# A state-space input product as one float32r product of stacked parts, its weights prepared by a side task of its own

## The chip, the cores and the metric

The kernel runs on one core of a Trainium2 chip. The metric is the device time of one execution in microseconds (us), the median of a few runs. A matrix product on TensorE (PE) can take float32 operands, or float32r operands, which are float32 values rounded to fewer bits; a float32 matmul leaves two records in the trace, a float32r matmul one.

## The reference, cut to what matters

Two transformer-like blocks of width 2048 work on 256 tokens. The first has a feed-forward part (`ffn1`), then a mixer made of a state-space branch (64 groups of 16 channels, each driving 64 complex states) and an attention branch, then a second feed-forward part. The second block follows it. The part that changes is the input of the state space:

```
u32 = u.reshape(Bsz, S, N_SSM_GROUPS, SSM_GROUP)
bu_re = jnp.einsum('bsgh,gph->sbgp', u32, bb_re)
bu_im = jnp.einsum('bsgh,gph->sbgp', u32, bb_im)
_, _, s_re, s_im = lax.associative_scan(_ssm_combine, (a_re_t, a_im_t, bu_re, bu_im), axis=0)
y = einsum(s_re, c_re) - einsum(s_im, c_im) + d * u32
```

Here `u` is the last quarter of the columns of `hn @ w_in`, 256 tokens by 1024 channels.

## The kernel before

Nearly all of the time goes to large products with weights that stream from memory. Each float32 operand is split into two float32r parts, hi and lo, and each product is the sum of three: hi by hi, hi by lo, lo by hi (`gemm`, lines 247 to 249 with the activations stationary, 255 to 257 with the weights stationary). The weights go through a pipeline by units of 128x1024: SyncE loads `raw`, ScalarE (ACT) writes `whi` (line 106), VectorE (DVE) writes `wlo` (line 116). When `gemm` takes a unit for use, it first puts the rounding of the unit four places on into ACT's queue and the `wlo` of the unit three places on into DVE's queue. So DVE is never more than three whole units ahead of PE.

Everything else is written as side tasks, Python generators that issue some instructions and then yield. After each unit `gemm` calls `tick`: the tick number rises by one, deferred functions that are due run, and each side task in the list goes on while the sum of yielded costs stays under a budget (`share`). A yield of `(cost, lag)` also keeps the task asleep for `lag` ticks. All engines take their instructions strictly in the order in which this recording issues them. `finish(task)` runs a task to its end with no product between its steps.

The names that matter here:

- `early` is a chain of side tasks that runs under `ffn1`; behind `ffn1` stands `K.finish(*early)`, and then the products with `w_in` start, first the two for `uT` (line 993 writes it, scaled, from PSUM), then those for `qT`, `kT`, `vt`.
- `next_norm` works on the end of `ffn1`: it spills `h` by two POOL (GpSimd) DMAs for each quarter (line 913), and transposes it (`tr`, line 304) two ticks later.
- `ssm_states` is a side task, spawned behind the two `uT` products. For 16 steps `jp` it multiplies 2 x 128 states: its products `bu` (line 701) take 32 rows of `uT` by 32 rows of the weights `sB`, in plain float32; DVE turns them (lines 705 to 709), scans (714) and turns back (719 to 723), POOL adds (725, 726), and every second step `out` multiplies by C (`sy`, line 684).
- `attend1` is the attention side task, ahead of `ssm_states` in the list. It takes eight pairs of heads: scores `ap` (757), `aS` (761 to 769), transposes `apt` (779) into `aPT` (780), `ao` (790).
- Behind the context's products (`ctx_columns`, whose side tasks write `cky` and `ckt`) stands `attn_half(0)`, four ticks of products, and then `K.finish(ssm)`.
- The pool `m4` has ten buffers of 128x1024 floats, and all these tasks share it: in `ssm_states` `rot` (for this step and the next), `ssw` and `sst` of this step, and up to two older `ssw`, in all up to six; in attention and its neighbours `aS` (two), `aPT`, `cky` and `ckt`, in all five.

Of the kernel before, what the change touches and what calls it, by code (L numbers as in the profile page):

```python
# [7 lines left out]
F32 = mybir.dt.float32  # L8
F32R = mybir.dt.float32r
I32 = mybir.dt.int32  # L10
AF = mybir.ActivationFunctionType
# [5 lines left out]
P = 128  # L17
D = 2048
T = 256
# [513 lines left out]
            yield 1800  # L533


def mod_vectors(K):
    nc = K.nc
    K.cs = K.c("cs", (P, 2, 16))
    nc.gpsimd.dma_start(K.cs[:, 0], K.a["c_x"])
    nc.gpsimd.dma_start(K.cs[:, 1], K.a["c_ctx"])  # L540
    yield 0, 4
    nc.scalar.activation(K.cs[:], K.cs[:], AF.Silu)
    K.modT = K.c("modT", (P, 2, 2, 16))
    K.gate = K.dram.tile([1, D], F32, name="gate")
# [65 lines left out]
def ctx_norm(K):  # L610
    nc, v = K.nc, K.nc.vector
    K.cnorm = K.dram.tile([2, P, D], F32, name="cnorm")
    for t in range(2):
        x = K.b8("ctx")
        nc.gpsimd.dma_start(x[:], K.a["ctx"][t * 128:t * 128 + 128, :])
        yield 0, 3
        mv, r = layer_stats(K, x, "cn")
        yield 3500
        v.tensor_scalar(x[:], x[:], mv[:, 0:1], r[:], op0=OP.subtract, op1=OP.mult)
        nc.gpsimd.dma_start(K.cnorm[t], x[:])  # L620
        yield 1200
# [39 lines left out]
def ssm_states(K, uT):  # L661

    nc, v, a = K.nc, K.nc.vector, K.a
    B, C, E = {}, {}, {}

    def fetch(jp):
        if jp >= 16:
            return
        if jp % 2 == 0:
            kt = jp // 2  # L670
            B[kt] = K.t1("sB", (P, 2, 128))
            nc.gpsimd.dma_start(B[kt][:], a["s_b"][kt])
            C[kt] = K.t1("sC", (P, 2, 4, 32))
            for i in range(2):
                nc.gpsimd.dma_start(C[kt][:, i], K.cfold[i, :, 4 * kt:4 * kt + 4, :])
        E[jp] = K.m4("rot", (P, 2, 2, 256))
        nc.gpsimd.dma_start(E[jp][:].rearrange("p a b c -> p (a b c)"), K.rot[jp])

    def out(kt, ws):
        p = K.ps("sy")  # L680
        for ri in range(2):
            for j in range(4):
                q = 32 * j
                nc.tensor.matmul(p[q:q + 32, :256], C[kt][:, ri, j], ws[j // 2][:, ri, j % 2], start=ri == 0, stop=ri == 1,
                                 skip_group_check=True)
        v.scalar_tensor_tensor(uT[:, kt, :], uT[:, kt, :], K.ssd[:, kt:kt + 1], p[:, :256], op0=OP.mult, op1=OP.add)

    fetch(0)
    yield 0, 2
    ws = []  # L690
    for jp in range(16):
        kt, half = divmod(jp, 2)
        fetch(jp + 1)
        c, e = E[jp][:, 0], E[jp][:, 1]
        w, t = K.m4("ssw", (P, 2, 2, 256)), K.m4("sst", (P, 2, 2, 256))
        bs = [K.ps("bu", (P, 2, 256)) for j in range(2)]

        for ri in range(2):
            for j in range(2):
                q = 32 * (2 * half + j)  # L700
                nc.tensor.matmul(bs[j][:, ri], B[kt][q:q + 32, ri], uT[q:q + 32, kt, :], start=ri == 0, stop=True,  # L701
                                 skip_group_check=True)
        for j in range(2):
            b = bs[j]
            v.tensor_tensor(w[:, :, j], b[:], c[:, j][:, None, :].to_broadcast([P, 2, 256]), op=OP.mult)
            v.tensor_tensor(t[:, :, j], b[:], e[:, j][:, None, :].to_broadcast([P, 2, 256]), op=OP.mult)
            yield 1200
        v.tensor_sub(w[:, 0], w[:, 0], t[:, 1])
        v.tensor_add(w[:, 1], w[:, 1], t[:, 0])
        yield 1500  # L710
        for ri in range(2):
            for j in range(2):
                m = K.mag[:, 2 * jp + j:2 * jp + j + 1].to_broadcast([P, 256])
                v.tensor_tensor_scan(w[:, ri, j], m, w[:, ri, j], 0.0, op0=OP.mult, op1=OP.add)
            yield 1350
        if len(ws) == 2:
            out(kt - 1, ws)
            ws = []
        v.tensor_tensor(t[:, 0], c, w[:, 0], op=OP.mult)
        v.tensor_tensor(t[:, 1], e, w[:, 0], op=OP.mult)  # L720
        yield 1200
        v.tensor_tensor(w[:, 0], e, w[:, 1], op=OP.mult)
        v.tensor_tensor(w[:, 1], c, w[:, 1], op=OP.mult)
        yield 1200
        nc.gpsimd.tensor_add(w[:, 0], t[:, 0], w[:, 0])
        nc.gpsimd.tensor_sub(w[:, 1], w[:, 1], t[:, 1])
        del E[jp]
        ws.append(w)
        yield 100
    yield 0, 3  # L730
    out(7, ws)
    yield 300, 2
# [199 lines left out]
def constants1(K):  # L932
    nc, a = K.nc, K.a
    yield 0, 6
    for name, shape in (("ones", (P, 1)), ("mask1", (P, 384)), ("halfpi", (P, 1)), ("ssd", (P, 8)), ("glub", (P, 8)),
                        ("gain_ssm", (P, 8)), ("gain_attn", (P, 8)), ("convw", (P, 4, 16))):
        t = K.c(name, shape)
        nc.gpsimd.dma_start(t[:], a[name])
        setattr(K, name, t)


def block1(K):
    nc, v, a = K.nc, K.nc.vector, K.a
    kx = list(range(16))
    h = [K.b8(f"h{t}") for t in range(2)]
    constants(K)
    for n in range(4):
        for t in range(2):
            c = slice(n * 512, n * 512 + 512)
# [21 lines left out]
            K.defer(2 * n + 1, lambda n=n, t=t: N.add(t, n, h[t][:, n * 512:n * 512 + 512]))  # L971
    K.defer(8, lambda: R.update(n1=N.done(D)))
    K.share = 1060.0
    early = [K.spawn(chain(constants1(K), mod_vectors(K), ctx_norm(K), ssm_prep(K), mod_rows(K, (0, 1), (0, 1))))]


    K.hspill = K.dram.tile([2, P, D], F32, name="hspill")
    xT2 = {}
# [7 lines left out]
    uT, qT, kT = (K.b8(n, (P, 8, 256)) for n in ("uT", "qT", "kT"))  # L986
    vt = K.b8("vt", (P, 2, 1024))

    def keepT(dst, i):
        def ev(acc):  # L990
            for q in range(2):
                o = dst[:, 4 * i + 2 * q:4 * i + 2 * q + 2, :]
                v.tensor_tensor(o, acc[:, q].rearrange("p (a b) -> p a b", a=2), R["rb"][:, None, :].to_broadcast([P, 2, 256]),
                                op=OP.mult)
        return ev

    for dst, n0 in ((uT, 3072), (qT, 0), (kT, 1024)):
        for i in range(2):
            K.gemm("T", "w_in", kx, n0 + 512 * i, 512, xT2, keepT(dst, i))
        if dst is uT:  # L1000
            ssm = K.spawn(ssm_states(K, uT))
    cT = {}
# [861 lines left out]
def cols(g,n): return np.ascontiguousarray(np.asarray(g).reshape(n,128).T)  # L1864
# [7 lines left out]
def small(I):  # L1872
    f=np.float32
    a={"x":I["x"][0],"ctx":I["ctx_2"][0]}
    a["ident"]=np.eye(128,dtype=f); a["ones"]=np.ones((128,1),f)
    t=np.arange(256)[:,None]; s=np.arange(256)[None]; d=t-s
    c=((d>=0)&(d<=128)).astype(int)+((d>=0)&(d%4==0))+((d>=0)&(d%16==0))
    m=np.where(c>0,8*np.log(np.maximum(c,1)),-1e30).astype(f)
    a["mask1"]=np.ascontiguousarray(np.concatenate([m[:128,:128],m[128:]],1))
    a["steps"]=np.broadcast_to(np.arange(256,dtype=f),(128,256)).copy(); a["halfpi"]=np.full((128,1),np.pi/2,f)  # L1880
    a["gains"]=np.ascontiguousarray(np.stack([cols(I[n][0],16) for n in("ffn1_norm","mix_norm","ffn2_norm")],1))
    a["ssd"]=cols(I["ssm_d"][0],8); a["glub"]=cols(I["ssm_b_glu"][0],8)
    a["gain_ssm"]=cols(I["ssm_out_norm"][0],8); a["gain_attn"]=cols(I["attn_out_norm"][0],8)
    a["convw"]=np.ascontiguousarray(np.stack([cols(w,16) for w in I["conv_w_2"][0]]+[cols(I["conv_b_2"][0],16)],1))
    st=lambda x: np.ascontiguousarray(x.reshape(32,128).T)
    a["s_lr"]=st(I["ssm_a_re"][0]); a["s_li"]=st(I["ssm_a_im"][0])
    a["s_ld"]=st(np.repeat(I["ssm_log_dt"][0],64))
    for n,k in(("s_cre","ssm_c_re"),("s_cim","ssm_c_im")):
        z=np.zeros((2,64,32,2,16),f)
        C=I[k][0].reshape(32,2,16,64)  # L1890
        for g in range(2): z[g,:,:,g,:]=C[:,g].transpose(2,0,1)
        a[n]=z.reshape(128,1024)
    z=np.zeros((8,4,2,16,2,2,64),f)
    for q,k in((0,"ssm_b_re"),(1,"ssm_b_im")):
        Bm=I[k][0].reshape(8,4,2,64,16)
        for g in range(2): z[:,:,g,:,q,g,:]=Bm[:,:,g].transpose(0,1,3,2)
    a["s_b"]=z.reshape(8,128,2,128)
    a["c_x"]=cols(I["c_2"][0],16); a["c_ctx"]=cols(I["c_ctx_2"],16)
    a["b_mod"]=I["b_mod_2"][0][None]; a["w_mod"]=I["w_mod_2"][0]
    return a  # L1900
# [47 lines left out]
```

## Time and profile before

| | us |
|---|---|
| median of 3 runs | 3184.89 (3184.13 to 3186.52) |
| profiled execution, its own time | 3183.86 |
| span of its trace | 3182.1 |
| PE busy | 3160.6 (99%) |
| DVE busy | 2227.1 (70%) |
| ACT busy | 1508.0 (47%) |
| POOL busy | 266.0 (8%) |

The span is the time from the first to the last instruction in the trace; 1.8 us of the execution's own time lie around it. Busy time of PE includes overlap of pipelined matmuls, so it tells that PE hardly ever waits, not that it could not be faster.

### The profile page before, as it was taken

The numbers are of one execution on the slowest core, as the hardware profiler recorded it, in microseconds if no ns is written. First come the engines' busy times: TensorE is split into PE (matmuls) and PEld (weight loads), VectorE is DVE, ScalarE is ACT, GpSimd is POOL, SyncE is SP. The second block draws the span as 40 slices with busy tenths as digits, with TensorE's granted clock in tenths as the row PEclk, the third lists the DMA queues.
The fourth block names the chain that finished last, engine by engine and source line by source line (L and its number), as shares of the span: only waits on it lengthen the run. The fifth ranks groups of instructions, "written<-read, shape, count | busy, mean of one in ns | idle before, by whom it ended". The sixth has DMA issues, their size and how long they took to land.

```text
span 3182.1 us, 41884 instructions
## 1 busy us (share of the span) xinstructions
PE 3160.6 (99%) x16096; PEld 2676.0 (84%) x16096; DVE 2227.1 (70%) x3160; ACT 1508.0 (47%) x1980; POOL 266.0 (8%) x411
## 2 busy tenths in 40 slices
PE   8999999999999999999999999999999999999999
PEld 7888888889988788888888888889988888888887
DVE  6768798795986887665766547767656875445567
ACT  5574444444357455544444444545544444444443
POOL 1000000000231321000000000000001110000001
PEclk9999999999999999999999999999999999999999
DMA  7678677776564565565876556554445555655663
GB/s 262 241 270 285 238 272 264 259 262 212 201 231 151 185 244 184 208 206 191 306 256 237 191 192 228 206 197 174 150 161 172 182 185 202 231 182 199 220 233 133
DMA packets 117144, 684.32 MB, mean 215 GB/s; under 512 B 15611, under 2 KB 15899, under 8 KB 52171
## 3 DMA queue, kind: packets, MB, share of 16 engines
q1 hardware_dynamic: 95616, 610.90, 53.8%
q0 software_dynamic: 21328, 70.74, 6.5%
q8 instruction: 126, 2.06, 0.3%
q14 instruction: 74, 0.61, 0.1%
HBM read 646.41 MB, written 35.18 MB: 214 GB/s over the span
## 4 chain that ended last, share of the span: by engine, by line
PE 96%; DVE 2%; ACT 1%; DMA 1%; issue 0%; POOL 0%; DVEq 0%; SPq 0%; ACTq 0%; POOLq 0%
PE acc L247 27%; PE acc L249 26%; PE acc L248 26%; PE acc L255 3%; PE acc L256 3%; PE acc L257 3%; PE tr L304 1%; PE mN L1467 1%; PE o2p L1381 1%; PE s L1359 1%; DVE wlo L116 1%; DMA raw<-w_ffn_w_gate 1%; PE bu L701 0%; PE pt L1371 0%; PE acc L281 0%; PE cp L1246 0%
## 5 line engine op out<-in xcount | busy, mean ns | idle before, releaser
L116 DVE TENSOR_TENSOR wlo<-raw,whi 128x1024 fp32r<-128x1024 f32 (+2 forms) x1072 | 1300.1, 1222 | 514.0 <-PE acc L248 402.1
L106 ACT ACTIVATE whi<-raw 128x1024 fp32r<-128x1024 f32 (+2 forms) x1072 | 1112.5, 1044 | 1131.6 <-PE acc L249 898.4
L247 PE MATMUL acc<-whi,xTh 128*128 128x512 f32 (+1 forms) x1472 | 570.6, 388 | 2.0 <-ACT xTh L313 2.0
L248 PE MATMUL acc<-wlo,xTh 128*128 128x512 f32 (+1 forms) x1472 | 568.0, 386 | 0.7 <-DVE wlo L116 0.7
L249 PE MATMUL acc<-whi,xTl 128*128 128x512 f32 (+1 forms) x1472 | 567.9, 386 | 0.3 <-DVE xTl L319 0.3
L247 PE MATMUL acc<-whi,uT2h 128*128 128x512 f32 (+2 forms) x992 | 387.4, 390 | 0.0
L249 PE MATMUL acc<-whi,uT2l 128*128 128x512 f32 (+2 forms) x992 | 380.9, 384 | 0.0
L248 PE MATMUL acc<-wlo,uT2h 128*128 128x512 f32 (+2 forms) x992 | 380.4, 383 | 0.0
L247 PEld LDWEIGHTS acc<-whi,xTh 128*128 128x128 f32 x1472 | 277.1, 188 | 56.9 <-ACT xTh L313 2.8
L249 PEld LDWEIGHTS acc<-whi,xTl 128*128 128x128 f32 x1472 | 277.0, 188 | 53.3 <-DVE xTl L319 0.6
L248 PEld LDWEIGHTS acc<-wlo,xTh 128*128 128x128 f32 x1472 | 277.2, 188 | 52.9 <-DVE wlo L116 1.9
L247 PE MATMUL acc<-whi,gTh 128*128 128x512 f32 x688 | 269.6, 392 | 1.2 <-DVE h L404 1.2
L249 PE MATMUL acc<-whi,gTl 128*128 128x512 f32 x688 | 268.3, 390 | 0.0
L248 PE MATMUL acc<-wlo,gTh 128*128 128x512 f32 x688 | 268.1, 390 | 0.0
L247 PEld LDWEIGHTS acc<-whi,uT2h 128*128 128x128 f32 x992 | 186.6, 188 | 37.2 <-issue 2.5
L249 PEld LDWEIGHTS acc<-whi,uT2l 128*128 128x128 f32 x992 | 186.4, 188 | 36.8
L248 PEld LDWEIGHTS acc<-wlo,uT2h 128*128 128x128 f32 x992 | 186.7, 188 | 35.1
L572 DVE SCALAR_TENSOR_TENSOR macc<-mraw,cs,macc 128x1024 f32<-128x1024 f32 x160 | 205.2, 1282 | 4.9 <-DMA mraw<-w_mod 4.9
L247 PEld LDWEIGHTS acc<-whi,gTh 128*128 128x128 f32 x688 | 129.3, 188 | 27.7 <-ACT whi L106 1.6
L249 PEld LDWEIGHTS acc<-whi,gTl 128*128 128x128 f32 x688 | 129.2, 188 | 26.9
L248 PEld LDWEIGHTS acc<-wlo,gTh 128*128 128x128 f32 x688 | 129.3, 188 | 26.2
L247 PE MATMUL acc<-whi,wTh 128*128 128x512 f32 (+1 forms) x384 | 148.2, 386 | 0.0
(549 smaller groups left out, 4431.4 us busy)
## 6 DMA issues: line engine op xcount, KB each, us to landing
raw<-w_w_in SPq DMA_DIRECT2D x192, 1024.0 KB, 4.9
raw<-w_ffn_w_gate SPq DMA_DIRECT2D x80, 1024.0 KB, 5.1
raw<-w_ffn_w_up SPq DMA_DIRECT2D x80, 1024.0 KB, 4.9
raw<-w_ffn_w_down SPq DMA_DIRECT2D x80, 1024.0 KB, 4.9
mraw<-w_mod SPq DMA_DIRECT2D x96, 512.0 KB, 6.4
raw<-w_w_out SPq DMA_DIRECT2D x28, 1024.0 KB, 4.9
rot<-rot POOLq DMA_DIRECT2D x32, 512.0 KB, 5.2
raw<-w_w_branch_b SPq DMA_DIRECT2D x16, 1024.0 KB, 4.8
```

Source lines behind the costliest of these rows:

```text
L106: K.nc.scalar.activation(hi[:, :nu * w], raw, AF.Copy)
L116: K.nc.vector.tensor_sub(lo[:, :n], raw, hi[:, :n].bitcast(F32))
L247: nc.tensor.matmul(o, xh[:, ts], wh, start=first, stop=False)
L248: nc.tensor.matmul(o, xh[:, ts], wl, start=False, stop=False)
L249: nc.tensor.matmul(o, xl[:, ts], wh, start=False, stop=last)
L255: nc.tensor.matmul(o, wh[:, ns], xh, start=first and n % 2 == 0, stop=False, **sk)
L256: nc.tensor.matmul(o, wh[:, ns], xl, start=False, stop=False, **sk)
L257: nc.tensor.matmul(o, wl[:, ns], xh, start=False, stop=last, **sk)
L304: nc.tensor.transpose(p[:, o:o + 128], src(kt, t), self.ident[:])
L572: v.scalar_tensor_tensor(accs[row][:], w[:], K.cs[:, row, kt:kt + 1], accs[row][:], op0=OP.mult, op1=OP.add)
L1359: nc.tensor.matmul(p[:], l[:, t * 128:t * 128 + 128], kk[:, r], start=i == 0, stop=i == 2)
L1381: nc.tensor.matmul(p[:, :128], PT[:, t, s * 128:s * 128 + 128], va[:, s, g * 128:g * 128 + 128], start=s == 0, stop=s == 3)
```

## The change

`ssm_inputs_prep` is a second early side task. It sleeps 60 ticks, then takes the weights of the input product, now laid out as three copies of 32 rows by 8192 columns, in eight chunks of 96x1024: a POOL DMA loads `bx`, ACT rounds it to `bz` (all three row blocks hi), DVE overwrites the middle block by lo, and a POOL DMA stores `bz` to `bst` in memory. `keep_u` splits `uT` into `uh` and `ul` after each of its two products and stores them to `ust` in memory. `fetch` then loads for each step a tile `us` of `m4` that holds u (hi, hi, lo in rows 0, 32 and 64) and the weights (hi, lo, hi), with four POOL DMAs, in place of the one for `sB`. The product has 96 rows in float32r; each of its two halves is issued just ahead of its DVE work. The first product comes five ticks after the first fetch, where it was two.

```
+def ssm_inputs_prep(K):
+    nc, v = K.nc, K.nc.vector
+    K.bst = K.dram.tile([96, 8192], F32R, name="bst")
+    yield 0, 60
+    for c in range(8):
+        cs = slice(c * 1024, c * 1024 + 1024)
+        x, z = K.m4("bx", (96, 1024)), K.m4("bz", (96, 1024), F32R)
+        nc.gpsimd.dma_start(x[:], K.a["s_b"][:, cs])
+        yield 0, 4
+        nc.scalar.activation(z[:], x[:], AF.Copy)
+        yield 0, 1
+        v.tensor_sub(z[32:64], x[32:64], z[32:64].bitcast(F32))
+        nc.gpsimd.dma_start(K.bst[:, cs], z[:])
+        yield 1200, 8
...
-            B[kt] = K.t1("sB", (P, 2, 128))
-            nc.gpsimd.dma_start(B[kt][:], a["s_b"][kt])
...
+        U[jp] = K.m4("us", (96, 2, 512), F32R)
+        for i in range(3):
+            nc.gpsimd.dma_start(U[jp][32 * i:32 * i + 32, 0].rearrange("r (j t) -> r j t", j=2),
+                                K.ust[i // 2, jp // 2, jp % 2].rearrange("j r t -> r j t"))
+        nc.gpsimd.dma_start(U[jp][:, 1], K.bst[:, jp * 512:jp * 512 + 512])
...
     fetch(0)
-    yield 0, 2
+    yield 0, 5
...
-        bs = [K.ps("bu", (P, 2, 256)) for j in range(2)]
-        for ri in range(2):
-            for j in range(2):
-                q = 32 * (2 * half + j)
-                nc.tensor.matmul(bs[j][:, ri], B[kt][q:q + 32, ri], uT[q:q + 32, kt, :], start=ri == 0, stop=True,
-                                 skip_group_check=True)
         for j in range(2):
-            b = bs[j]
+            b = K.ps("bu", (P, 2, 256))
+            for ri in range(2):
+                o = (2 * j + ri) * 128
+                nc.tensor.matmul(b[:, ri], U[jp][:, 1, o:o + 128], U[jp][:, 0, j * 256:j * 256 + 256], start=ri == 0,
+                                 stop=True, skip_group_check=True)
...
-    early = [K.spawn(chain(constants1(K), mod_vectors(K), ctx_norm(K), ssm_prep(K), mod_rows(K, (0, 1), (0, 1))))]
+    early = [K.spawn(chain(constants1(K), mod_vectors(K), ctx_norm(K), ssm_prep(K), mod_rows(K, (0, 1), (0, 1)))),
+             K.spawn(ssm_inputs_prep(K))]
...
+        def parts():
+            ks = slice(4 * i, 4 * i + 4)
+            hi, lo = (K.m4(n, (P, 4, 256), F32R) for n in ("uh", "ul"))
+            nc.scalar.activation(hi[:], uT[:, ks], AF.Copy)
+            v.tensor_sub(lo[:], uT[:, ks], hi[:].bitcast(F32))
+            for x, z in enumerate((hi, lo)):
+                nc.gpsimd.dma_start(K.ust[x, ks].rearrange("k a j r t -> (a j r) k t"), z[:])
```

Where `ffn1` ends, POOL's queue before holds the last spills of `h` and then the first fetch of `ssm_states` (`sB`, `sC`, `rot`). Now it holds this behind the same spills (a name's number tells the buffer):

```order
L931 DMA hspill_133<-h0_83 128x512
L931 DMA hspill_133<-h1_84 128x512
L544 DMA bx_5868<-s_b 96x1024
L549 DMA bst_180<-bz_5869 96x1024
L544 DMA bx_5874<-s_b 96x1024
L549 DMA bst_180<-bz_5875 96x1024
L544 DMA bx_5880<-s_b 96x1024
L549 DMA bst_180<-bz_5881 96x1024
L544 DMA bx_5886<-s_b 96x1024
L549 DMA bst_180<-bz_5887 96x1024
L1027 DMA ust_5896<-uh_6155 128x4x256
```

Four of the eight chunks of `ssm_inputs_prep` stand here, each store ahead of the next chunk's load. On DVE the same place, between the last row of the norm of `h` and the copy of `rb`, reads before:

```order
L332 SCALAR_TENSOR_TENSOR n2ry<-n2rt,n2ry 128x2
L116 TENSOR_TENSOR wlo<-raw,whi 128x1024 x2
L319 SCALAR_TENSOR_TENSOR xTl<-tr,gains,xTh 128x256 x4
L116 TENSOR_TENSOR wlo<-raw,whi 128x1024 x3
L631 COPY rb<-row 128x256
```

and now:

```order
L332 SCALAR_TENSOR_TENSOR n2ry<-n2rt,n2ry 128x2
L548 TENSOR_TENSOR bz<-bx,bz 32x1024 x4
L116 TENSOR_TENSOR wlo<-raw,whi 128x1024
L319 SCALAR_TENSOR_TENSOR xTl<-tr,gains,xTh 128x256 x4
L116 TENSOR_TENSOR wlo<-raw,whi 128x1024 x4
L648 COPY rb<-row 128x256
```

The four subtractions of the chunks now stand ahead of the next `wlo`; on ACT the four copies stand likewise ahead of the next `whi`. The last place is the end of `ssm_states`, in `attn_half(0)`. DVE before, from the last row of the attention's norm (`sqA`) to the last use of `sy`:

```order
L332 SCALAR_TENSOR_TENSOR sqAry<-sqArt,sqAry 128x2
L116 TENSOR_TENSOR wlo<-raw,whi 128x1024
L722 TENSOR_TENSOR ssw<-rot,ssw 128x512
L723 TENSOR_TENSOR ssw<-rot,ssw 128x512
L116 TENSOR_TENSOR wlo<-raw,whi 128x1024 x3
L686 SCALAR_TENSOR_TENSOR uT<-uT,ssd,sy 128x256
```

and now:

```order
L332 SCALAR_TENSOR_TENSOR sqAry<-sqArt,sqAry 128x2
L116 TENSOR_TENSOR wlo<-raw,whi 128x1024
L732 SCALAR_TENSOR_TENSOR ssw<-mag,ssw 128x256 x2
L116 TENSOR_TENSOR wlo<-raw,whi 128x1024
L732 SCALAR_TENSOR_TENSOR ssw<-mag,ssw 128x256 x2
L116 TENSOR_TENSOR wlo<-raw,whi 128x1024
L737 TENSOR_TENSOR sst<-rot,ssw 128x512
L738 TENSOR_TENSOR sst<-rot,ssw 128x512
L116 TENSOR_TENSOR wlo<-raw,whi 128x1024
L740 TENSOR_TENSOR ssw<-rot,ssw 128x512
L741 TENSOR_TENSOR ssw<-rot,ssw 128x512
```

The last scans and turns of the state space moved from ahead of the norm to behind it, and the last two turns from behind one `wlo` to behind four. On PE the last `sy` stands where it stood, behind the fourth tick of `attn_half(0)`.

## Rows read from the trace of the kernel before

**Rows 1.** The page: busy time of PE; chain that ended last, by engine.
```profile
PE 3160.6 (99%) x16096; PEld 2676.0 (84%) x16096; DVE 2227.1 (70%) x3160; ACT 1508.0 (47%) x1980; POOL 266.0 (8%) x411
PE 96%; DVE 2%; ACT 1%; DMA 1%; issue 0%; POOL 0%; DVEq 0%; SPq 0%; ACTq 0%; POOLq 0%
```

**Rows 2.** Waits of PE, whole run: us in total, times, longest.
```profile
PE ap L757 <- ACT ckt L851: 4.0, 2, 2.4
PE ap L757 <- DVE sst L706: 1.0, 1, 1.0
PE ao L790 <- ACT aPT L780: 0.7, 1, 0.7
```

**Rows 3.** Timeline of PE at the first input product: start us, us, instruction.
```profile
794.94 0.28 PE L257 MATMUL acc<-xTh,wlo 128*128 128x256 f32 x1
795.14 1.13 PE L701 MATMUL bu<-uT,sB 32*128 32x256 f32 x8
796.21 0.38 PE L255 MATMUL acc<-xTh,whi 128*128 128x256 f32 x1
796.43 0.28 PE L256 MATMUL acc<-xTl,whi 128*128 128x256 f32 x1
796.55 0.28 PE L257 MATMUL acc<-xTh,wlo 128*128 128x256 f32 x1
```

**Rows 4.** Instructions of tile bu: ns min/median/max, first and last start.
```profile
L701 PE MATMUL bu<-uT,sB x128: 373/375/479, 795.1 to 1138.3; 32*128 32x256 f32 x128
```

**Rows 5.** Timeline of PE where ffn1 ends.
```profile
739.06 0.39 PE L249 MATMUL acc<-whi,gTl 128*128 128x512 f32 x1
739.28 0.28 PE L255 MATMUL acc<-xTh,whi 128*128 128x256 f32 x1
...
745.03 1.04 PE L304 MATMUL tr<-ident,h 128*128 128x128 f32 x8
```

**Rows 6.** Timeline of POOL where ffn1 ends; in brackets idle time before, its releaser.
```profile
740.47 1.14 POOL L913 DMA_DIRECT2D hspill<-h  x2 [9.92 <-DVE h L404]
741.60 0.54 POOL L672 DMA_DIRECT2D sB<-s_b  x1
```

**Rows 7.** Timelines of ACT and DVE behind ffn1: one unit's whi, one unit's wlo.
```profile
757.75 1.06 ACT L106 ACTIVATE whi<-raw 128x1024 fp32r<-128x1024 f32 x1 [2.07 <-PE acc L256]
757.87 1.23 DVE L116 TENSOR_TENSOR wlo<-raw,whi 128x1024 fp32r<-128x1024 f32 x1 [1.36 <-issue]
```

**Rows 8.** DMA issues, 795 to 900 us: KB each, median us to landing.
```profile
rot<-rot POOLq DMA_DIRECT2D x5, 512.0 KB, 4.3
sB<-s_b POOLq DMA_DIRECT2D x3, 128.0 KB, 2.4
```

**Rows 9.** The same, 738 to 800 us.
```profile
rot<-rot POOLq DMA_DIRECT2D x2, 512.0 KB, 5.4
```

**Rows 10.** Windows in attention: busy us (x) of PE, PEld, DVE, ACT, POOL; granted clock; DMA.
```profile
990.00:995.00 5.00, 3.37 (x29) 3.13 (x28) 4.01 (x10) 4.97 (x10) 1.23 (x1) 1.00 0.03 7
995.00:1000.00 5.00, 5.00 (x27) 4.67 (x27) 2.03 (x7) 4.27 (x12) 1.09 (x2) 0.66 0.86 289
```

**Rows 11.** Timeline of DVE at the end of the state space.
```profile
1151.09 1.27 DVE L714 TENSOR_TENSOR_SCAN ssw<-mag,ssw 128x256 f32<-128x256 f32 x2
...
1153.39 0.69 DVE L719 TENSOR_TENSOR sst<-rot,ssw 128x512 f32<-128x512 f32 x1
...
1154.59 0.16 DVE L657 TENSOR_SCALAR sqAms<-ssp 128x2 f32<-128x2 f32 x1
...
1157.97 0.69 DVE L722 TENSOR_TENSOR ssw<-rot,ssw 128x512 f32<-128x512 f32 x1
```

**Rows 12.** Timeline of POOL at the same place.
```profile
1158.81 1.74 POOL L725 TENSOR_TENSOR ssw<-sst,ssw 128x512 f32<-128x512 f32 x1 [6.39 <-DVE ssw L722]
1160.50 2.27 POOL L726 TENSOR_TENSOR ssw<-ssw,sst 128x512 f32<-128x512 f32 x1
```

**Rows 13.** Timeline of PE at the same place.
```profile
1161.36 0.39 PE L249 MATMUL acc<-whi,mixAl 128*128 128x512 f32 x1
1161.68 1.77 PE L684 MATMUL sy<-ssw,sC 128*32 128x256 f32 x16
1163.38 0.50 PE L247 MATMUL acc<-whi,mixAh 128*128 128x512 f32 x1
```

More of the change, by code (lines that the diff above doesn't have):

```diff
@@ L663, in ssm_states @@
     nc, v, a = K.nc, K.nc.vector, K.a
-    B, C, E = {}, {}, {}
+    U, C, E = {}, {}, {}
     def fetch(jp):
@@ L726, in ssm_states @@
         nc.gpsimd.tensor_sub(w[:, 1], w[:, 1], t[:, 1])
-        del E[jp]
+        del E[jp], U[jp]
         ws.append(w)
@@ L995, in keepT, with keep_u, both @@
         return ev
+    K.ust = K.dram.tile([2, 8, 2, 2, 32, 256], F32R, name="ust")
+    def keep_u(i):
+        ev = keepT(uT, i)
+        def parts():
[5 more added lines that the diff above has]
+                nc.gpsimd.dma_start(K.ust[x, ks].rearrange("k a j r t -> (a j r) k t"), z[:])
+        def both(acc):
+            ev(acc)
+            parts()
+        return both
     for dst, n0 in ((uT, 3072), (qT, 0), (kT, 1024)):
         for i in range(2):
-            K.gemm("T", "w_in", kx, n0 + 512 * i, 512, xT2, keepT(dst, i))
+            K.gemm("T", "w_in", kx, n0 + 512 * i, 512, xT2, keep_u(i) if dst is uT else keepT(dst, i))
         if dst is uT:
@@ L1896, in small @@
         for g in range(2): z[:,:,g,:,q,g,:]=Bm[:,:,g].transpose(0,1,3,2)
-    a["s_b"]=z.reshape(8,128,2,128)
+    z=z.reshape(16,2,32,256).transpose(2,0,1,3).reshape(32,8192)
+    a["s_b"]=np.ascontiguousarray(np.concatenate([z]*3))
     a["c_x"]=cols(I["c_2"][0],16); a["c_ctx"]=cols(I["c_ctx_2"],16)
```

## The prediction, as it went on record

> **What bounds the kernel now.** I read the page first: PE is busy for 99% of the span and holds 96% of the chain that ended last [rows 1]. So time comes back only where PE's stream gets shorter, and is lost only where PE waits. Then PE's waits: in the stretch that the change touches only attention makes PE wait, 4.0 + 1.0 + 0.7 = 5.7 us [rows 2]. Neither the end of ffn1 nor the end of the state space stands in that list. Then the timelines of PE, DVE and POOL at those two places, because the order of the changed program moves work there, and what matters is how far DVE and POOL run ahead of PE.
>
> **What the product gains.** Before, a group of eight records (four float32 matmuls) stands between a product that starts at 794.94 and the second one behind the group at 796.43 [rows 3]. Without the group these two would lie two ordinary steps of 0.12 us apart (796.43 to 796.55), so a group costs 1.49 - 0.24 = 1.25 us, and 16 groups (128 records [rows 4]) cost 20.0 us. After, a step has four float32r matmuls of 256 columns. The nearest row is the 128-row float32r matmul of 256 columns at 0.12 us a step; I take the same for 96 rows, 4 x 0.12 x 16 = 7.7 us, and a gain of 12.3 us. If the two pairs of a step, now issued apart, each cost another 0.12 us for entering and leaving, the gain is 8.5 us; its upper end is the whole 20.0.
>
> The rule that speaks against this edit: a record lasts 375 ns by its median [rows 4], so eight in line would be 3.0 us, but the eight span 1.13 us [rows 3], so they overlap. The Trainium skill, page "TensorE: Matmul & The Clock Gate", Part 3 on packing small matmuls, says that matmuls of 32 rows on different row groups run at the same time, and that one of 32 rows alone takes as long as one of 128. The old order alternates between two row groups, so by that rule the stacked product gives an overlap up; the trace agrees. Without the overlap the sum would promise 16 x (3.0 - 0.48) = 40 us.
>
> **What the burst behind ffn1 costs.** `ssm_inputs_prep` stands behind the long chain of early tasks and shares its budget, so only four of its eight chunks are through when ffn1 ends; `finish` issues the other four with no product between them. The rows of the order show four loads and four stores in turn on POOL, four copies on ACT ahead of the next `whi`, four subtractions on DVE ahead of the next `wlo`. POOL waits in line: its idle 9.92 us end with the `h` that its spill stores [rows 6]. So the store of a chunk waits for its subtraction, the next load waits behind that store, and four round trips follow one another. What is queued behind them on DVE is a `wlo`, and PE waits for that.
>
> Start: POOL is free at 741.6 [rows 6]. One trip is a load until it lands, a copy, a subtraction, and (three times) the issue of the store ahead of the next load, 0.54 us [rows 6]. Copy and subtraction work on 1024 columns like `whi` and `wlo`, 1.06 and 1.23 us [rows 7]; fewer partitions I take to save nothing. The load is 384 KB. POOL's loads of 128 and 512 KB land after 2.4 and 4.3 us [rows 8]; in line between them 384 KB is 3.7. So 741.6 + 4 x (3.7 + 1.06 + 1.23) + 3 x 0.54 = 767.2, and the `wlo` is there at 768.4.
>
> Without it PE has three whole units. Two of them take 745.03 - 739.28 = 5.75 us [rows 5], three 8.6; the eight transposes, 1.04 us [rows 5], now come behind the first unit, and two more matmuls don't need the `wlo`: PE stops at 739.28 + 8.6 + 1.04 + 0.24 = 749.2. The stall is 19.2 us. With loads at 2.4 us it is 14.0, at 5.4 us [rows 9] 26.0.
>
> The Trainium skill gives a price for such a load: "DMA: Bandwidth & Descriptors", section on the anatomy of one DMA on the SWDGE (gpsimd) path, has 2.0 us plus the bytes at 436 GB/s, an estimate of 2.9 us for 384 KB and a stall of 16 us. Its 3.2 us for 512 KB lies under the 4.3 of this trace, its 2.3 for 128 KB by the 2.4.
>
> **The clock.** After 1.6 us without work in 990 to 995, the next 5 us ran at a mean granted clock of 0.66, 1.2 GHz for part of them [rows 10]; 0.34 x 5 = 1.7 us lost. I count one such loss after the burst and one for the stalls below, 3.4 us; bounds 0 and 7.
>
> **What the later start costs at the end.** With three ticks more ahead of the first product the state space ends three ticks later, and `finish` stands at the same place. The four scans and two turns that DVE had done ahead of the attention's norm now come behind it. Before, DVE starts the norm at 1154.59 and the turn that POOL waits for ends at 1158.66 [rows 11]. The moved work (two pairs of scans at 1.27, two turns from 1153.39 to 1154.59: 3.7 us [rows 11]) only changes sides, but three more `wlo` of some 1.2 us now stand ahead of that turn, so it ends at 1162.3. POOL's two adds, 1.70 and 2.27 us [rows 12], end 3.6 us later too, at 1166.3 where it was 1162.8. PE had no slack: `sy` started at 1161.68 and the next product at 1163.38 [rows 13]. I take 3.5 us; 1.5 if DVE's head start absorbs part of it, 7 if the first add already holds PE.
>
> **What the new tiles cost in attention.** The state space held up to six of the ten `m4` buffers, attention and its neighbours want five; with `us` of this step and the next it is up to eight plus five. `attend1` comes first in the list, so the state space sleeps on its buffers while attention runs, and an `aS`, `aPT`, `cky` or `ckt` then waits for another one's release. No row shows such a wait. Bounds: -5.7, if the new order removes today's waits; and eight pairs of heads with the longest wait of today, 2.4 us [rows 2], 19. I take five pairs at the mean of today's two waits on `ckt`, 2.0 us [rows 2]: 10 us.
>
> **At nothing.** The four early chunks (4 x 1.06 us ACT, 4 x 1.23 us DVE) lie under ffn1's products, as do the 2 x 2 splits of `uT` under those of `w_in`: DVE's and ACT's units there end with idle time of 1.36 and 2.07 us [rows 7]. Uncovered, one would cost its 1.2 us. The loads of `us` replace `sB`; the three ticks, 8.6 us, cover the way of `uT` through memory. If they didn't, one more landing of 2.4 to 4.3 us would be added.
>
> **Sum.** Against the profiled execution's 3183.9: - 12.3 + 19.2 + 3.4 + 3.5 + 10 = 3207.7 us. That execution is 1.0 us under the median, so I predict 3209, slower by 0.75%. What this measurement can tell from no change is about 0.2%, 6.4 us.
>
> **Rivals.** (a) Attention absorbs the tiles, and the rest holds: 3199. For it: attention's waits depend on the order, and ACT and DVE have room. Against: eight plus five is well over ten. (b) Heavier: loads land after 5 us and attention pays 15 or more: 3219 to 3225. For it: the first load meets the weight loads [rows 9]. Against: with PE stopped those loads stop. (c) The gain is lost, because the 96-row product costs a group about what it did: 3221. Against: the weight products in float32r beside it go at 0.12. (d) Faster: the burst is hidden. If POOL sent all four loads off at once, the chain would be one landing, one copy and four subtractions, 741.6 + 3.7 + 1.06 + 4.9 + 1.2 = 752.5 against 749.2; a stall of 3.3 us, with (a)'s attention and the end as above about 3180, without the end's 3.5 and a clock loss 3176. It decides as soon as all stalls together stay under 12.3 us, which for the burst alone means trips under 4.8 us instead of 6.5. Against: POOL's wait for `h` [rows 6], and the stores stand between the loads.
>
> **Numbers.** Forecast (3203 to 3217) 0.60; (a) 0.18; (b) 0.13; (c) 0.04; (d) or an equal small stall 0.05. Faster by over 0.2% 0.03, within 0.2% 0.04, slower 0.93. The range 3196 to 3224 leaves out (d), and of (a) and (b) the ends.
>
> **What would show it.** In the profile after: PE idle for some 19 us behind the third unit of the first `w_in` product, released by `wlo`, with POOL, ACT and DVE taking turns through four chunks; granted clock under 1 right behind; groups of `bu` at 0.24 us a pair; PE waiting for POOL at the last `sy`; PE's waits in attention at about 15 us. I am wrong if the burst's trips overlap, if loads land well under 3 us, or if attention's waits stay at 5.7.

## The result, and the profile after

The changed kernel takes 3236.88 us (median of four runs, 3235.78 to 3239.78) against 3184.51 us of the kernel before on the same chip: a ratio of 1.0166, with a 95% interval of 1.0154 to 1.0177. The profiled execution took 3236.04 us, its span is 3234.2 us where it was 3182.1, and its mean granted clock is 0.991. So the change is slower by 52 us, the forecast was slower by 24: the sign was right, and the time lies 13 us above the range.

The page after, busy time of PE and the chain that ended last, against [rows 1]:

```profile
PE 3162.5 (98%) x16032; PEld 2677.6 (83%) x16032; DVE 2236.0 (69%) x3170; ACT 1518.4 (47%) x1990; POOL 310.4 (10%) x487
PE 90%; DVE 3%; issue 2%; DMA 2%; ACT 2%; POOL 1%; DVEq 0%; SPq 0%; ACTq 0%; POOLq 0%
```

PE's records are 64 fewer, its busy time is not less, since part of it ran at half clock, and 6% of the chain has gone from PE to others: PE waits. The waits of PE after (us in total, times, longest), against [rows 2], where the three of context and attention make 5.7 us:

```profile
PE acc L257 <- DVE wlo L116: 28.2, 1, 28.2
PE sy L705 <- POOL ssw L743: 6.1, 1, 6.1
...
PE ao L808 <- ACT aPT L798: 5.0, 2, 3.4
PE ap L775 <- ACT ckt L869: 5.0, 2, 2.6
...
PE ckp L868 <- DVE cky L844: 2.9, 1, 2.9
PE tr L1053 <- DMA cu<-cnorm: 2.6, 2, 2.0
```

Where the time went is read best by pairing the `acc` products, 14256 in either trace and in the same order, and taking for each the start after less the start before. Where this delay grows, time was lost. Worked out from the two traces, for the two spans' 52.1 us:

```
place                            start before   start after   delay   step
first units behind ffn1              745.83        747.69      1.86
behind the burst                     752.13        783.71     31.58   +29.7
half of the state space              919.36        943.54     24.18    -7.4
context and attention over          1049.28       1094.61     45.33   +21.2
last products before the end        1158.87       1199.92     41.05    -4.3
behind the end of the state space   1167.16       1218.31     51.15   +10.1
last acc product                    3169.33       3221.46     52.13    +1.0
```

Of the first 1.86 us, 1.82 are there after 73 us, where the two programs are still the same (the preparation begins at 260 us). The profiled executions of the other kernels lie -0.2 to 3.2 us from the one before at that place, so this part belongs to the execution and not to the change.

**The burst** is the one wait of 28.2 us. The timeline of POOL there (start us, us, instruction; in brackets idle time before and its releaser), against [rows 6]:

```profile
743.59 0.53 POOL L544 DMA_DIRECT2D bx<-s_b  x1
754.12 0.52 POOL L549 DMA_DIRECT2D bst<-bz  x1 [10.01 <-DVE bz L548]
754.63 0.51 POOL L544 DMA_DIRECT2D bx<-s_b  x1
762.18 0.51 POOL L549 DMA_DIRECT2D bst<-bz  x1 [7.03 <-DVE bz L548]
...
778.16 0.51 POOL L549 DMA_DIRECT2D bst<-bz  x1 [7.01 <-DVE bz L548]
```

and that of ACT, whose copy starts when a load has landed:

```profile
751.52 1.06 ACT L546 ACTIVATE bz<-bx 96x1024 fp32r<-96x1024 f32 x1 [7.99 <-DMA bx<-s_b]
759.58 1.06 ACT L546 ACTIVATE bz<-bx 96x1024 fp32r<-96x1024 f32 x1 [7.00 <-DMA bx<-s_b]
```

Four round trips, one behind the other, as forecast: store, load, copy, subtraction, store. A trip takes 8.0 us (754.12 to 762.18). Of it the load, from its issue to the copy, is 4.95 us (754.63 to 759.58); the first load took 7.93 (743.59 to 751.52). The windows of the burst (length; busy us of PE, PEld, DVE, ACT, POOL; granted clock; DMA share; GB/s), against [rows 10]:

```profile
740.00:760.00 20.00, 10.97 (x88) 10.57 (x86) 6.09 (x18) 2.82 (x6) 2.84 (x6) 0.87 0.51 158
760.00:780.00 20.00, 0.82 (x4) 0.82 (x5) 5.74 (x7) 6.13 (x10) 2.53 (x5) 0.50 0.33 89
```

PE stands still in the second window, and its granted clock is 0.50 there, 1.2 GHz. PE's products start again at 779.2, and up to 782.2 they take nearly twice as long (0.21 us a step, 0.12 behind it), which makes some 1.4 us of the step of 29.7.

**Context and attention** lose 21.2 us. PE's idle time in this stretch is 17.5 us of 151.07 where it was 5.7 of 129.92; much of the rest is half clock, for which see the part on the prediction. What makes PE late there is a step away from it. The waits of DVE between 950 and 1112 us:

```profile
DVE aS L779 <- DMA ck<-ckt: 12.3, 2, 7.4
...
DVE cky L839 <- ACT cky L838: 9.8, 4, 7.9
DVE aS L779 <- PE ao L810: 6.7, 2, 4.0
```

and in the kernel before, where DVE waits for no `ckt` and no `ao`, the only line of `aS`:

```profile
DVE aS L761 <- PE ap L757: 7.0, 4, 2.2
```

An `aS` reads neither `ckt` nor `ao`. By the program it can only wait for the `m4` buffer in which that `ckt` was, until its way to memory is over, or for the one of an `aPT` that `ao` still reads. The trace names who ended the wait, not the buffer. DVE takes its work in order, so all that stands behind the `aS` waits too. In the context POOL's queue does the same to the loads of `cu`: they stand behind the loads of the next step of the state space, and those behind adds that had waited for DVE:

```profile
938.90 2.27 POOL L744 TENSOR_TENSOR ssw<-ssw,sst 128x512 f32<-128x512 f32 x1
941.12 1.65 POOL L694 DMA_DIRECT2D us<-ust  x3
...
943.27 0.59 POOL L698 DMA_DIRECT2D rot<-rot  x1
943.83 2.19 POOL L1045 DMA_DIRECT2D cu<-cnorm  x4
```

The first of them goes out 7.3 us ahead of the first transpose (943.83 to 951.12), where it was 19.8 us (905.1 to 924.9). The transposes wait 2.6 us for `cu`, half clock follows (0.83 over 950 to 960), and the delay grows by 6 there (24.18 at the product that starts at 919.36 before, 30.23 at the one that starts at 933.60).

**The end of the state space.** DVE, POOL and PE, against [rows 11 to 13]:

```profile
1198.34 0.15 DVE L674 TENSOR_SCALAR sqAms<-ssp 128x2 f32<-128x2 f32 x1
...
1208.64 0.69 DVE L740 TENSOR_TENSOR ssw<-rot,ssw 128x512 f32<-128x512 f32 x1
```

```profile
1209.42 1.77 POOL L743 TENSOR_TENSOR ssw<-sst,ssw 128x512 f32<-128x512 f32 x1 [13.66 <-DVE ssw L740]
```

```profile
1211.24 1.08 PE L705 MATMUL sy<-ssw,sC 128*32 128x256 f32 x8 [6.05 <-POOL ssw L743]
```

From the norm's start to the end of POOL's first add there were 5.96 us (1154.59 to 1158.81 + 1.74), now there are 12.85 (1198.34 to 1209.42 + 1.77).

### The profile page after: what moved, and what is told of

It is laid out like the page before. It is cut to its first block, busy times and chain, and to the rows that moved or that the text cites. A ratio compares the mean times of both kernels' runs of the same rounds, so it can differ in the third digit from the quotient of the medians.

```text
span 3234.2 us, 41920 instructions
## 1 busy us (share of the span) xinstructions
PE 3162.5 (98%) x16032; PEld 2677.6 (83%) x16032; DVE 2236.0 (69%) x3170; ACT 1518.4 (47%) x1990; POOL 310.4 (10%) x487
## 4 chain that ended last, share of the span: by engine, by line
PE 90%; DVE 3%; issue 2%; DMA 2%; ACT 2%; POOL 1%; DVEq 0%; SPq 0%; ACTq 0%; POOLq 0%
PE acc L247 25%; PE acc L249 25%; PE acc L248 25%; PE acc L255 3%; PE acc L257 3%; PE acc L256 3%; PE tr L304 1%; DVE wlo L116 1%; PE mN L1504 1%; PE o2p L1418 1%; PE s L1396 1%; DMA raw<-w_ffn_w_gate 1%; PE pt L1408 0%; ACT whi L106 0%; PE acc L281 0%
## 5 line engine op out<-in xcount | busy, mean ns | idle before, releaser
L248 PEld LDWEIGHTS acc<-wlo,gTh 128*128 128x128 f32 x688 | 129.2, 188 | 26.3
```

The costliest lines, as they stand in the source:

```text
L248: nc.tensor.matmul(o, xh[:, ts], wl, start=False, stop=False)
```

## The experiments

The steps above name three suspects: the burst, the three ticks, the tiles. Theory at the start: the burst costs what the one wait shows, the ticks cost the end, and the tiles cost context and attention. The main rival: the ticks cost all that is behind ffn1, and the tiles nothing. The kernel before was measured again beside the runs, at 3185.2 to 3186.9 us, where it was 3184.5 beside the changed kernel; so each ratio is to the kernel before beside the run itself, and a difference to the changed kernel is good to some 2 us.

**Without a burst.** The preparation goes to the front of the list of side tasks.

```
-             K.spawn(ssm_inputs_prep(K))]
+             K.spawn(ssm_inputs_prep(K), first=True)]
```

> The changed kernel, with the preparation task put ahead of the long chain of early tasks in the list, so that all eight chunks are through while ffn1 still has products to run. If the burst behind ffn1 costs what the trace of the changed kernel shows (28.2 us of waiting for one wlo and some 1.4 us of half clock behind it), PE passes 800 us some 28 to 30 us earlier and the time is 3206 to 3210. Rival: the four chunks that move into ffn1 only move their cost, because ACT and DVE fall behind there; then the wait comes back in pieces within ffn1 and the time stays above 3220.

Measured: 3209.54 us, 1.0071 of before (1.0054 to 1.0087); 27.3 us less than the changed kernel. The wait of 28.2 us for `wlo` behind ffn1 is gone, and ffn1 with all eight chunks in it is about 1 us longer. In its place the first input products now wait for their loads:

```profile
PE bu L721 <- DMA us<-bst: 5.4, 2, 4.5
```

The store of `ul` ahead of them landed 12.9 us after its issue (8.3 in the changed kernel); the reason for this was not tried.

**Loads one chunk ahead.** The same burst, but each load is issued ahead of the store of the chunk before it.

```
+    load(0)
     for c in range(8):
+        load(c + 1)
-        nc.gpsimd.dma_start(x[:], K.a["s_b"][:, cs])
```

> The changed kernel, where each chunk's load is issued one chunk earlier, ahead of the store of the chunk before; loads, stores and arithmetic are the same in number. If the burst is a chain of round trips because a load stands behind a store that waits for its subtraction, two chunks share a trip and the wait for wlo falls from 28.2 to 11 to 16 us: 3221 to 3226. Rival: the transfers themselves set the pace (a load that lands after 4.9 us moves its 384 KB as fast as it can); then two loads at once land twice as late, the wait stays above 24 us and the time above 3232.

Measured: 3222.47 us, 1.0113 (1.0098 to 1.0128); 14.4 us less. PE's wait there and two lines of POOL's timeline:

```profile
PE acc L257 <- DVE wlo L116: 10.5, 1, 10.5
```

```profile
749.56 0.51 POOL L546 DMA_DIRECT2D bx<-s_b  x1
753.72 0.51 POOL L557 DMA_DIRECT2D bst<-bz  x1 [3.65 <-DVE bz L556]
```

The load of the first of the four chunks now lies ahead of the spills, and the stall has three loads left in it. They take 6.1, 5.0 and 5.0 us to their copies though the next one goes out before or just as one lands, and the stores follow one another by 4.7, 3.5 and 4.7 us in place of 8.0. So the stall is the chain of round trips, not the transfers' pace: overlapping loads don't land twice as late, and PE waits 17.7 us less.

**Why a load takes 4.95 us.** Each chunk's load fills 128 rows from one block of memory, 512 KB, instead of 96 rows, 384 KB.

```
-        nc.gpsimd.dma_start(x[:], K.a["s_b"][:, cs])
+        nc.gpsimd.dma_start(x[:], K.a["s_b"][r:r + 16, :].rearrange("r (b n) -> (r b) n", b=8))
```

> The changed kernel, but the load of each chunk of weights fills 128 rows of 1024 (512 KB) from one block of memory, not 96 rows (384 KB) from 96 places; the stacked weights are then wrong, only the burst is of interest. In the burst a load of 384 KB took 4.95 us from its issue to the copy, where 512 KB of rot took 4.3. If the 96 rows or their places make the load slow, 512 KB in 128 rows land after 4.3 to 4.6 us and the trip falls from 8.0 to 7.4 to 7.7 us. Rival: the load is slow because it stands right behind a store in the queue, or for its bytes; then a trip takes 8.0 to 8.7 us.

Measured: 3236.62 us (two runs), 1.0161 (1.0143 to 1.0180); the trips are 8.5 to 8.9 us, the loads longer:

```profile
759.66 0.52 POOL L550 DMA_DIRECT2D bst<-bz  x1 [7.46 <-DVE bz L549]
760.21 0.53 POOL L545 DMA_DIRECT2D bx<-s_b  x1
768.29 0.52 POOL L550 DMA_DIRECT2D bst<-bz  x1 [7.54 <-DVE bz L549]
```

So 128 rows from one block are no quicker; nothing here speaks for the 96 rows as the cause. That the load goes with its bytes and its place behind a store fits, but the two were not told apart.

**Two ticks.** The changed kernel with the old distance between the first loads and the first product.

```
-    yield 0, 5
+    yield 0, 2
```

> The changed kernel, with the first product two ticks behind the first loads as before, not five. If the stall at the end of the state space belongs to the three ticks, the waits of sy on POOL (6.1 us) and the half clock at 1208.9 to 1215.7 us go, and the time falls by 9 to 10 us to 3227. If the waits in attention belong to the later start too and not to the new tiles, a further 10 to 16 us go: 3211 to 3218. Rival: the three ticks cover the way of uT through memory; then PE waits once at the first product, for 2 to 6 us, and the gain is that much smaller.

Measured: 3219.79 us, 1.0108 (1.0093 to 1.0123); 17.1 us less. Nearly all of the loss at the end and in attention leaves with the ticks (1.5 and 2.9 us are left), and DVE waits for no `ckt` on its way to memory; but the first product pays:

```profile
PE bu L721 <- DMA us<-bst: 9.1, 1, 9.1
```

This spoke for the rival, that the ticks cost everything. The next three runs split it.

**The tiles alone.** The kernel before, with one more `m4` buffer a step, filled by four loads on POOL's queue. Nothing is computed from it; one DVE copy of two columns reads it (not in the cut).

```
+        U[jp] = K.m4("us", (96, 2, 512))
+        for i in range(3):
+            nc.gpsimd.dma_start(U[jp][32 * i:32 * i + 32, 0], K.rot[jp, 32 * i:32 * i + 32, 0:512])
+        nc.gpsimd.dma_start(U[jp][:, 1], K.rot[jp, 0:96, 512:1024])
```

> The kernel before with the new tiles alone: each step of the state space also takes one more m4 buffer and fills it by four loads on POOL's queue of the sizes of the changed kernel; one DVE copy of two columns a step reads it, and nothing is computed from it. Product, weights, start and order are those of before. If the new tiles and their loads cost the time in the transposes of the context (6 us) and in attention (16 us), the time is 3199 to 3209. Rival: these 22 us belong to the three ticks, which shift the state space against attention; then it is within 4 us of 3184.5.

Measured: 3190.80 us, 1.0016 (1.0006 to 1.0025). The tiles alone, with their loads, cost about 4 us, not 22. My theory fell.

**The ticks alone.** The kernel before with five ticks.

> The kernel before with the first product five ticks behind the first loads, not two; nothing else. One theory: the later start by itself shifts the state space against the context and attention, and moves work behind ffn1's successor at the end; then the 6 us at the transposes of the context, the 16 us in attention and the 10 us at the end, which all left with the three ticks in the run before, come in here too, and the time is 3207 to 3217. Rival: it takes both, tiles that fill the m4 buffers and the later start; then here there is only the end, 3 to 6 us: 3188 to 3192.

Measured: 3194.25 us, 1.0027 (1.0017 to 1.0037). The ticks alone cost 9 us, and the paired products put 7.7 of them at the end (the delay is 1.59 ahead of it and 9.32 behind):

```profile
PE sy L684 <- POOL ssw L725: 6.1, 1, 6.1
```

The main rival fell too: without the tiles, context and attention lose 1.5 us.

**Both together**, and still nothing else of the change. The copy of two columns stands at a step's first product here.

> The kernel before with the two suspects together, and with nothing else of the change: one more m4 buffer a step, filled by four loads on POOL's queue and read by one DVE copy of two columns at the first product, and five ticks instead of two. Nothing is computed from the new tiles. The tiles alone cost 3.9 us and the ticks alone 8.6. Theory: the two act together, because with the later start a step's tiles are still held when attention asks for its own; then the 6 us at the transposes of the context and most of the 16 us in attention come in, with DVE waiting in line for a ckt that is on its way to memory: 3205 to 3218. Rival: they only add, and the 22 us need the product's own order too (two pairs of matmuls a tick apart): 3196 to 3201.

Measured: 3213.10 us, 1.0086 (1.0072 to 1.0100): 27 us, where the sum of the two is 13. PE loses 18 us in context and attention and 10.3 at the end, as in the changed kernel, and the waits are the same ones:

```profile
PE ckp L856 <- DVE cky L832: 2.9, 1, 2.9
...
PE tr L1022 <- DMA cu<-cnorm: 1.4, 1, 1.4
```

```profile
DVE aS L767 <- DMA ck<-ckt: 12.2, 2, 7.3
```

So neither the tiles nor the ticks cost attention its time, but the two together do. The product itself is not needed for it. A tile brings a held buffer and four loads on POOL's queue, and no run has one without the other.

**Buffers held for half as long.** The changed kernel, five ticks, with a step's inputs fetched behind the scans of the step before.

```
+        inputs(jp + 1)
         v.tensor_tensor(t[:, 0], c, w[:, 0], op=OP.mult)
```

> The changed kernel, still with five ticks, but with the input tile of a step fetched half a step later, behind the scans of the step before (three ticks ahead of its product), and so held for half as long. If the number of m4 buffers that are held makes attention wait, the waits of DVE for ckt on its way to memory go and the time falls by 8 to 20 us: 3217 to 3229. Rival: what counts is POOL's longer queue or the shift itself; both stay, and the time stays above 3232, or rises where a load now comes late for its product.

Measured: 3250.39 us, 1.0201 (1.0187 to 1.0215): 13.5 us more than the changed kernel, so the theory's range of time failed, and the rival's rise by late loads came. DVE's waits for a `ckt` on its way to memory are gone all the same, as the theory of the buffers has it, with all the loads still there; PE's for `cky` too. Of the other runs, these waits of DVE take 6.7 to 12.3 us wherever new tiles meet three ticks or five; with the ticks alone, or the tiles at two ticks, there is none, and with one tick one of 1.6 us. But POOL's queue issues the late loads later still, behind its adds and stores, and PE waits for them:

```profile
PE bu L725 <- DMA us<-bst: 30.2, 6, 10.0
```

For the total this one tells nothing, since a new wait hides what was won.

**The first loads early.** The inputs of the first eight steps need only the first half of `uT`, so the first step's loads can be issued one `w_in` product sooner; then two ticks are enough.

```
-    yield 0, 5
+    yield 0
+    yield 0, 2
...
+            if n0 == 3072 and i == 0:
+                next(ssm)
```

> The changed kernel with the loads of the first state-space step issued behind the first of the two w_in products that make uT (they need only its half), and the first product two ticks behind the second, as before. With two ticks alone the first product waited 9.1 us for us, with half clock behind it. If that wait is the way through memory, it goes, and the time is 3208 to 3211, with nothing of the 32 us in context, attention and end. Rival: POOL now waits for the stores of the first half ahead of other work, or the longer life of one buffer costs as much: 3216 or more.

Measured: 3207.68 us, 1.0073 (1.0060 to 1.0086), 29.2 us less than the changed kernel. The wait of 9.1 us has gone. The burst is still there (26.3 us of waiting for `wlo`); what is left of PE's waits behind it is near what was there before:

```profile
PE ap L776 <- ACT ckt L870: 4.0, 2, 2.3
...
PE sy L705 <- POOL ssw L745: 0.9, 1, 0.9
```

**Without a burst and with early loads**, two ticks.

> The changed kernel with both: the preparation ahead of the long chain of early tasks (no burst behind ffn1) and the first loads behind the first half of uT with two ticks. If the burst and the later start are all that the change costs, the gain of the product is left, 10 to 12 us, less up to 5 us for the tiles: 3175 to 3182, faster than the kernel before by 0.15 to 0.35%. Rival: the tiles and the chunks inside ffn1 take the gain: 3185 or more.

Measured: 3181.14 us, 0.9987 (0.9978 to 0.9996): faster than the kernel before, by 4 us. That is a third of the product's 12 us. In the profiled run, the slowest of the eleven (3183.96 us), the paired products show 3.75 us lost by the end of ffn1 (2.66 of it in the first 73 us, where the runs differ by as much among themselves), 1.6 at the end of the state space, and this wait, among others:

```profile
PE bu L722 <- ACT aff L1154: 2.4, 1, 2.4
```

**One tick and three**, in this last kernel.

> The kernel of the last but one comparison that was faster than before (preparation ahead, first loads behind the first half of uT), with one tick instead of two ahead of the first product. What is left of waits there after the state space (0.9 us of sy on POOL) would go, and nothing else is near a limit: 3178 to 3182, level with two ticks. Rival: attention and state space fall into another step with each other by one tick, and waits of several us come or go in attention: outside 3175 to 3186.

Measured: 3181.27 us, 0.9986 (0.9976 to 0.9995), level with two.

> The same with three ticks. One theory: the cost of the later start grows with each tick, a third of the 29 us that five ticks cost (with the loads early or not) for each: 3189 to 3192. Rival: the end grows by a step of about 3 us a tick, but attention's waits jump in only where the state space's tiles meet attention's, and three ticks stay below that: 3181 to 3186, with PE's waits in attention as they were and no wait of DVE for a ckt on its way to memory.

Measured: 3192.09 us, 1.0020 (1.0012 to 1.0029). That is at the upper edge of the theory's range, but the cost doesn't grow evenly, since the tick from one to two is free and that from two to three costs 11 us; nor is there a step only at the end, since DVE's wait for a `ckt` on its way, none with two ticks and 1.6 us with one, is back with the third:

```profile
DVE aS L780 <- DMA ck<-ckt: 6.7, 1, 6.7
```

## Why the prediction was wrong

Direction and places were right: a burst behind ffn1 with four trips in a row, `m4` buffers in attention, the end of the state space. Its terms were too small. The steps of the table hold the half clock: 29.7 behind the burst where 19.2 and 1.7 of clock were taken, 21.2 in context and attention where 10 and 1.7 were, 10.1 at the end where 3.5 were. They fell short by 8.8, 9.5 and 6.6 us, 25 of the 28 us by which the sum missed the profiled execution; most of the rest are the first 1.9 us and the last 1.0, which belong to no term.

**The product: right.** The timeline of PE in the kernel with early loads:

```profile
824.46 0.28 PE L257 MATMUL acc<-xTh,wlo 128*128 128x256 f32 x1
824.58 0.64 PE L722 MATMUL bu<-us 96*128 96x256 f32 x4
825.06 0.29 PE L255 MATMUL acc<-xTh,whi 128*128 128x256 f32 x1
...
890.99 0.40 PE L722 MATMUL bu<-us 96*128 96x256 f32 x2
891.23 0.28 PE L255 MATMUL acc<-xTh,whi 128*128 128x256 f32 x1
```

Four of 96 rows take 0.48 us, 0.12 each, as the 128-row products beside them and as taken from [rows 3]; a pair apart takes 0.24 (890.99 to 891.23), so it costs nothing for entering or leaving. So the gain is 16 x (1.25 - 0.48) = 12.3 us. Rival (c) is out. What the Trainium skill says in "TensorE: Matmul & The Clock Gate", Part 3, of 32-row products on different row groups at one time agrees with it: the overlap of [rows 3] was given up, and a gain of 12.3 us was left, not one of 40.

**The burst: mechanism right, its landing mis-sized.** The step that failed reads "in line between them 384 KB is 3.7". The four loads took 7.93 + 4.95 + 4.83 + 4.92 = 22.6 us in place of 14.8; copy, subtraction and the handing on took 2.60 a trip (759.58 to 762.18) in place of 2.29, 1.2 in all. The start came 2.0 us later and PE's stop 1.8 (751.0). Together 28.2 in place of 19.2. The 3.7 came from loads that have no store right ahead of them. For the first load rival (b) had named the weight loads, and the DMA share was 0.51 around it; but two spills of `h` stand right ahead of it too, and no run parts the two. Its price was put too low. "With PE stopped those loads stop" held for the other three. The price of the Trainium skill, "DMA: Bandwidth & Descriptors", section on the anatomy of one DMA, an estimate of 2.9 us, is farther off still.

**Attention: mechanism right, count and price wrong.** The step that failed is "I take five pairs at the mean of today's two waits", with an upper end of 19 us. The stretch lost 21.2, some 6.6 of it by half clock. The bound was built from waits of PE for `ckt`; but a buffer wait stands on DVE, lasts up to 7.4 us, until a store has landed, and holds up whatever DVE has in line. And I named attention alone, where the context ahead of it loses 6 of the 21. The runs also add what I hadn't seen: it needs the later start. With two ticks the tiles cost the kernel before 4.0 us there (the delay grows from 0.72 to 4.69).

**The end: place right, cost wrong.** The step that failed is "the moved work only changes sides", which lets DVE start the norm 3.7 us earlier against PE. From the norm to POOL's first add the chain grew by 6.9 us, near the 7.3 that follow from the prediction's steps (3.7 earlier, 3.6 later). But the norm started 2.7 us later against PE (1198.34 - 1154.59 = 43.75, where PE's delay was 41.05). The timelines of DVE show why; before, and then now:

```profile
1147.65 1.22 DVE L116 TENSOR_TENSOR wlo<-raw,whi 128x1024 fp32r<-128x1024 f32 x1
```

```profile
1188.78 1.23 DVE L116 TENSOR_TENSOR wlo<-raw,whi 128x1024 fp32r<-128x1024 f32 x1 [0.41 <-ACT whi L106]
...
1191.25 2.31 DVE L116 TENSOR_TENSOR wlo<-raw,whi 128x1024 fp32r<-128x1024 f32 x1
```

The first line of each is the same unit's `wlo`, the 389th of the trace. It starts 41.13 us later than before, and PE's delay there is 40.76: DVE has won no head start, though the moved work is not ahead of it. From there to the norm DVE works without idle time 6.94 us before and 9.56 us now. Where four scans and two turns stood (3.6 us), the state space, three ticks behind, now has two turns back of one step and the turning of the next (5.1 us), and the `wlo` at 1191.25 takes some 1.1 us longer than the others, while POOL's adds run (1190.76 to 1194.72). So what left this place was replaced by more, and nothing of the 3.7 us was won. With the ticks alone the same stretch takes 9.56 us too (1147.53 to 1157.09), but DVE comes to that `wlo` 1.7 us ahead of PE's delay, and the end costs 7.7 there and 10.1 here, where 3.5 was taken and 7 was the end of the bounds.

**The clock: counted too seldom.** The step that failed is "one such loss after the burst and one for the stalls below". Against the one loss of [rows 10] the changed kernel has six spells at a granted clock of 0.50, 1.2 GHz: the one of the burst, one in the context, three in attention, one at the end of the state space (both traces have one more in the last microseconds, with PE all but idle). The windows around the last five:

```profile
950.00:960.00 10.00, 8.28 (x47) 5.77 (x48) 4.60 (x7) 5.16 (x9) 3.22 (x6) 0.83 0.84 273
1025.00:1045.00 20.00, 16.32 (x97) 13.81 (x98) 8.69 (x25) 13.45 (x33) 1.84 (x3) 0.83 0.29 92
1065.00:1085.00 20.00, 13.32 (x55) 9.01 (x54) 8.67 (x21) 12.97 (x26) 2.19 (x3) 0.74 0.38 132
1205.00:1220.00 15.00, 8.79 (x38) 5.70 (x37) 11.62 (x19) 9.15 (x19) 3.01 (x2) 0.77 0.48 171
```

Half of PE's busy time in a spell is what it costs, an estimate: 1.4 us behind the burst, 8.3 in context and attention (1.7 before), 2.2 at the end, 11.9 in all where it was 1.7. So the clock took some 10 us more than before; 3.4 was the forecast, 7 the end of its bounds. These us lie inside the steps above.

**At nothing.** That early chunks and splits lie under products holds, nearly (about 1 us with all eight in ffn1). The three ticks do cover the way of `uT` through memory: with five PE waits 0.4 us, with two 9.1, not the 2.4 to 4.3 that I had named as its price.

With the steps of the table, which add up to the spans' difference by construction, the sum is: 3183.9 + 1.9 ahead of ffn1's end + 29.7 - 7.4 + 21.2 - 4.3 + 10.1 + 1.0 = 3236.1. The two negative terms are for the most part the product's gain: 14 of its 16 groups stand there before, 10.8 us at 0.77 each. The other two lie in context and attention.

Open is what lengthens the landing by 1.2 us in the quiet part of the burst, whether the held buffer alone would do in attention without the longer queue on POOL, and which single buffer first closes the way in attention between the second and the third tick.

## What to carry to other kernels

A burst of side work in an in-order queue costs its number of round trips times the landing time in that place; issue the loads ahead of the stores, or spread the task under products by its place in the list. Two edits that each cost little can meet: more buffers with their loads and a later start cost 4 and 9 us alone and 27 together, so price them together, by who holds the pool when the next user asks. Count the half clock behind each new wait as well: here it was a fifth of the loss. And look for what a wait needs before it is bought off with a delay: half of the input was there one product sooner, and the three ticks, with some 29 us, were not needed.

## What the runs showed of the hardware

A load of 384 KB on POOL's queue right behind a store took 4.8 to 4.95 us to the copy that waits for it, with the DMA share at 0.33, and one of 512 KB 5.4 to 5.8 (760.21, and the copy at 765.69), where 512 KB of `rot` had landed after 4.3 [rows 8]. Stacked 96-row float32r products of 256 columns go one each 0.12 us with nothing lost where they follow or precede 128-row ones. A `wlo` on DVE that ran while POOL added took 2.31 us where others took 1.2 (1191.25; before, one of 2.32 at 1140.56 beside POOL's add at 1140.10).
